# A MoE whose expert blocks add their rows to their tokens' rows in DRAM

## The chip, the cores and the metric

The kernel runs on one core of one Trainium2 chip. The metric is the device time of one execution in microseconds. A core has a matrix engine (TensorE, here PE), a vector engine (VectorE, DVE), an activation engine (ScalarE, ACT), a general engine (GpSimd, POOL) and a sequencer that only starts transfers (SyncE, SP), each with its own instruction queue that runs in order, and 16 DMA engines that all transfers share.

## The reference

Two layers of one trunk work on 768 tokens of width 1024 (256 of context, 512 latent). Each layer has a mixer (a convolution and a state-space scan, in parallel, with one input and one output projection) and then a hierarchical mixture of experts. Only the second is touched by the change:

```python
def hier_moe(h, p):
    g_sel = jnp.argmax(t @ p["w_rg"] + p["b_rg"], axis=-1)          # one of 4 groups
    ...
    top_v, top_i = lax.top_k(jax.nn.softmax(e_logits, axis=-1), MOE_TOPK)   # 2 of 4 experts
    w_sel = g_prob * top_v / jnp.sum(top_v, axis=-1, keepdims=True)
    ...
    def expert(acc, ew):
        wg, wu, wd, cw = ew
        hid = jax.nn.silu(t @ wg) * (t @ wu)
        return acc + (cw[:, None] * (hid @ wd)).astype(acc.dtype), None
```

So each token goes to two of 16 experts, and its two results are added, gated and added to the residual. All data is float32. The second layer's MoE works on the 512 latent tokens alone, and a last RMSNorm gives the output.

## The kernel before

The kernel is written with a framework that puts each engine's instructions in an order by a simulated timeline of its own, and sets the semaphore waits. So the order on an engine follows neither the source alone nor the measured times.

**The expert blocks.** Layer 0 has 768 tokens, layer 1 has 512. A routing stage computes on DVE for each expert the list of its tokens. `CAPS` gives each of the 16 experts a fixed capacity of rows, so that the blocks can be laid out ahead: three experts of a fixed place (128 rows in layer 0, 96 in layer 1) and 13 whose places are filled by the order of their loads (208 down to 48 rows, and 160 down to 40). A block has at most 128 rows; there are 21 blocks with 1936 rows in layer 0 and 17 with 1308 rows in layer 1. What doesn't fit goes through a loop (`tc.For_i(0, nrun)`, L1508), which in this run is entered with zero passes.

For each block an indirect transfer on POOL (`gather`, L1257) brings the tokens' rows of 1024 floats from `h2d` in DRAM, two blocks ahead. PE turns them and multiplies them with the expert's gate and up weights, ACT and DVE apply the SwiGLU and the token's weight, and `down` multiplies with the down weights. Each weight is split in a high and a low part: ACT casts (L1248), and DVE or POOL subtracts (L1249; on POOL for the tiles `C` and `HL`, the second pair of an expert's six pieces). SP loads the six pieces of 512 KB of each expert (`raw`).

**The results.** `down` leaves a block's result `y` in SBUF, and a plain transfer on ACT's queue (L1330) puts it into `ysl`, the list of all result rows in the order of the blocks. Each token has two slots in that list, `slotc`, which the routing computes at its end (`sh`, `row`, `own`: L1410 to L1418). Behind the blocks, `fetch` (L1499) brings for each of the chunks of 128 tokens the two result rows of each token by an indirect transfer on POOL, the second with addition onto the first. In layer 1 both are added in the transfer onto a copy of the residual (ACT L1486). Three of them are issued ahead of the loop (`EARLY`), the others behind it. `combine` multiplies the sum with the gate, adds it to the residual `X1` and stores it (layer 0), or hands it to the last norm (layer 1: ACT L1574, POOL L356, DVE L1576, store L1577). In layer 0 the normed chunks are turned and enter layer 1's input projection (PE L483 to L485), whose weights `wp` SP loads, ACT casts and DVE or POOL subtracts (L465, L466).

**The routing.** DVE puts the token numbers and weights into their places by one-hot products: L1396 and L1399 compare, L1402 multiplies, PE sums (L1406), and `token_weight` (L1219 to L1221) turns that into `idx`, the list that the gathers read. Empty places have token 0 and weight 0.

## Time and profile before

| | |
|---|---|
| times of three runs | 1352.81, 1356.26, 1366.07 us |
| median | 1356.26 us |
| the profiled execution's own time | 1361.08 us |
| its span, first to last instruction | 1359.4 us |
| busy: PE, DVE, ACT, POOL | 80%, 67%, 42%, 44% |
| mean granted clock of PE | 0.902 |
| DMA moved | 258.79 MB, mean 190 GB/s |

The busy shares are averages over stages that are unlike: the mixers, the routing, the expert blocks and the two places where a layer ends. Idle time of an engine is read together with what ended it, which the views put in square brackets behind a row. A DMA's row on POOL or SP is its issue; when its data has landed is told by who waited for it, or by the view of transfers.

### The profile page before, as it was taken

Reading aid. Unit: us, or ns where it says so; the run is one execution under the profiler, and the core shown is the slowest. Engines: PE = TensorE matmul, PEld = TensorE weight load, DVE = VectorE, ACT = ScalarE, POOL = GpSimd, SP = SyncE. Lnnn points to the kernel's source line nnn. Section 1 sums busy time; section 2 is a strip of 40 time slices with the busy share of each in tenths; the row PEclk is TensorE's granted clock in tenths of the full one; section 3 lists DMA queues with packets and bytes.
Section 4 is the critical chain, followed back from the end, with each engine's and each line's share of the span. In section 5 each row is a group of like instructions: output and inputs, shape, how many; then the busy total and the mean of one; then the engine's idle time right before and its main releaser. Section 6 shows DMA issues by size and latency. Waiting matters only on the chain. (4 is left out here: it accounts for less than half of the span.)

```text
span 1359.4 us, 19509 instructions
## 1 busy us (share of the span) xinstructions
...
## 2 busy tenths in 40 slices
...
DMA  8855434513443194999856666022594363989856
GB/s 256 274 164 197 142 106 122 169 48 105 159 131 103 68 333 157 340 351 315 277 186 183 214 189 201 11 68 96 186 328 144 111 196 109 348 298 314 304 157 158
DMA packets 120733, 258.79 MB, mean 190 GB/s; under 512 B 16108, under 2 KB 61786, under 8 KB 115514
## 3 DMA queue, kind: packets, MB, share of 16 engines
...
q10 hardware_dynamic: 7429, 19.89, 3.9%
...
## 5 line engine op out<-in xcount | busy, mean ns | idle before, releaser
L466 POOL TENSOR_TENSOR t<-wp,t 128x1024 fp32r<-128x1024 f32 (+1 forms) x36 | 109.6, 3047 | 134.0 <-ACT t L465 108.8
L724 DVE SCALAR_TENSOR_TENSOR acc<-v,cwcol,acc 128x504 f32<-128x504 f32 (+19 forms) x176 | 136.2, 802 | 0.6
L1249 POOL TENSOR_TENSOR C<-raw,wraw 128x1024 fp32r<-128x1024 f32 x28 | 74.4, 2671 | 113.0 <-ACT wraw L1248 67.5
L483 PE MATMUL mm<-HL,t 128*128 128x512 f32 (+1 forms) x272 | 110.2, 408 | 15.4 <-ACT ad L438 7.1
L1248 ACT CAST wraw<-raw 128x1024 fp32r<-128x1024 f32 x92 | 94.5, 1047 | 43.4 <-DMA raw<-in_w_down_dram 16.3
L485 PE MATMUL mm<-HL,t 128*128 128x512 f32 (+1 forms) x272 | 107.6, 396 | 1.7 <-POOL t L466 1.7
L484 PE MATMUL mm<-HL,t 128*128 128x512 f32 (+1 forms) x272 | 107.3, 395 | 0.2 <-DVE HL L378 0.2
L1249 POOL TENSOR_TENSOR HL<-raw,HL 128x1024 fp32r<-128x1024 f32 x24 | 63.5, 2659 | 78.7 <-ACT HL L1248 78.6
L356 POOL TENSOR_TENSOR rstd<-ms,mhalf 128x1 f32<-128x1 f32 (+3 forms) x29 | 24.3, 838 | 150.4 <-DVE ms L354 150.4
L653 DVE SCALAR_TENSOR_TENSOR t<-t,pcol,t 128x772 f32<-128x772 f32 (+1 forms) x64 | 87.1, 1360 | 2.0
L483 PE MATMUL sm<-wraw,t 128*128 128x256 f32 (+8 forms) x304 | 88.0, 290 | 0.0
L484 PE MATMUL sm<-C,t 128*128 128x256 f32 (+8 forms) x304 | 85.8, 282 | 2.2 <-DVE C L1249 1.9
L485 PE MATMUL sm<-wraw,t 128*128 128x256 f32 (+8 forms) x304 | 85.7, 282 | 0.0
L483 PE MATMUL mm<-t,HL 128*128 128x256 f32 x256 | 76.3, 299 | 8.3 <-ACT t L645 2.6
L1257 POOL DMA_INDIRECT t<-h2d,idx x38 | 55.3, 1456 | 59.0 <-DVE cw L1221 17.1
L465 ACT CAST t<-wp 128x1024 fp32r<-128x1024 f32 (+1 forms) x40 | 42.0, 1053 | 90.5 <-DMA wp<-in_w_in_dram 40.0
L483 PE MATMUL sm<-HL,t 128*128 128x256 f32 (+8 forms) x272 | 78.7, 289 | 1.8 <-ACT HL L1248 1.7
L484 PE MATMUL sm<-HL,t 128*128 128x256 f32 (+8 forms) x272 | 77.2, 284 | 1.9 <-DVE HL L1249 1.9
L485 PE MATMUL sm<-HL,t 128*128 128x256 f32 (+8 forms) x272 | 77.2, 284 | 0.0
L483 PEld LDWEIGHTS mm<-HL,t 128*128 128x128 f32 x272 | 53.8, 199 | 33.3 <-issue 7.4
L485 PE MATMUL mm<-t,HL 128*128 128x256 f32 x256 | 75.0, 294 | 0.1
L484 PE MATMUL mm<-t,HL 128*128 128x256 f32 x256 | 74.5, 292 | 0.0
(472 smaller groups left out, 3388.7 us busy)
## 6 DMA issues: line engine op xcount, KB each, us to landing
...
```

Of the source, the lines that this page charges most:

```text
L356: G.tensor_tensor(r[:, :n], ms[:, :n], mhalf[:, :n], op=OP.pow)
L465: S.copy(hi, t)
L466: eng.tensor_sub(lo, t, hi)
L483: T.matmul(dst, lh, rh, start=(k == 0), stop=False)
L484: T.matmul(dst, lh, rl, start=False, stop=False)
L485: T.matmul(dst, ll, rh, start=False, stop=(k == K8 - 1))
L653: V.scalar_tensor_tensor(xa[:, :n], xpt[:, tap:tap + n], col, xa[:, :n], op0=OP.mult, op1=OP.add)
L724: eng.scalar_tensor_tensor(da, sa, tapc(k, ct), da, op0=OP.mult, op1=OP.add)
L1248: highs.append(S.copy(hi, r))
L1249: eng.tensor_sub(lo, r, hi)
L1257: gathered.append(G.indirect_dma_start(out=xg[:n], out_offset=None, in_=h2d, in_offset=bass.IndirectOffsetOnAxis(ap=icol[:n], axis=0)))
```

## The change

Each block adds its result to its tokens' rows in DRAM at once. `acc_d` has a row for each token, and 128 rows ahead of them for empty places: `idx` now counts from there, so token t is row 128 + t and an empty place of partition p is row p, which no other place of that block has. In layer 0 `acc_d` is filled with zeros while the mixer runs (eight stores of 512 KB on SP, one of them for the empty rows of `h2d`), in layer 1 with the residual `X1` (four stores on SP, when the routing's logits are done). `down` ends in `scatter`, an indirect transfer on POOL with addition. The fetches, `ysl`, `slotc` and the steps that computed it are gone, and `combine` loads a chunk of `acc_d` by a plain transfer on SP. In the loop the result is scattered too, in place of a product that picked tokens, and the weights lie in other tiles.

```diff
     G.iota(tokid[:, 0], pattern=[[0, 6]], base=0, channel_multiplier=1, allow_small_or_imprecise_dtypes=True)
-    G.iota(tokid[:, 1], pattern=[[1, 6]], base=0, channel_multiplier=0, allow_small_or_imprecise_dtypes=True)
+    G.iota(tokid[:, 1], pattern=[[1, 6]], base=1, channel_multiplier=0, allow_small_or_imprecise_dtypes=True)
     zrow = const.tile([P, 8], F32, name="zrow")
...
     av = const.tile([P, 2, 16], F32, name="av")
-    block0, capv, rowsh = [const.tile([P, 2, 16], F32, name=n) for n in ("block0", "capv", "rowsh")]
+    block0, capv = [const.tile([P, 2, 16], F32, name=n) for n in ("block0", "capv")]
     for l in range(2):
...
             G.memset(capv[:, l, j:j + 1], float(n))
-            G.memset(rowsh[:, l, j:j + 1], float(P * b - row))
...
-    slotc = const.tile([P, 2, 6], I32, name="slotc")
+
+    h2d, acc_d = [dram.tile([P + NT, D], F32, name=n) for n in ("h2d", "acc_d")]
     for l in range(2):
...
         ln_fill()
+        if not last:
+            z = main.tile([P, D], F32, name="t4", bufs=8)
+            V.memset(z, 0.0)
+            nc.sync.dma_start(out=h2d[0:P, :], in_=z)
+            for i in range(7):
+                nc.sync.dma_start(out=acc_d[i * P:(i + 1) * P, :], in_=z)
...
                         V.scalar_tensor_tensor(x[h], x[h], self.r[:, j:j + 1], self.sr[:, h], op0=OP.mult, op1=OP.add)
-                        nc.scalar.dma_start(out=h2d[i * P:(i + 1) * P, h * 512:(h + 1) * 512], in_=x[h])
+                        nc.scalar.dma_start(out=h2d[(i + 1) * P:(i + 2) * P, h * 512:(h + 1) * 512], in_=x[h])
...
             pr.norm()
+            if last:
+                for i in (i0, i0 + 1):
+                    nc.sync.dma_start(out=chunk(acc_d, i + 1), in_=X1[:, :, i, :])
         mix_stack.close()
...
         size = [min(P, n - j) for *_, n in items for j in range(0, n, P)]
-        NB, nrow = len(size), sum(size)
+        NB = len(size)
         nblk = NB + M_x
         nst = NB * P
-        ysl = dram.tile([nrow + 1, D], F32, name=f"ysl{l}")
-        nc.sync.dma_start(out=ysl[0:1, :].rearrange("o (p k) -> (o p) k", p=P), in_=zrow)
...
             tid = rt(f"tid{n}", n)
-            V.tensor_scalar(tid, p3[:, :, 1], 128.0, None, op0=OP.mult)
+            V.tensor_scalar(tid, p3[:, :, 1], 0.0, tokid[:, 0, 0:1], op0=OP.is_equal, op1=OP.mult)
+            V.scalar_tensor_tensor(tid, p3[:, :, 1], 128.0, tid, op0=OP.mult, op1=OP.add)
             V.tensor_tensor(idx, tid, p3[:, :, 0], op=OP.add)
...
                 S.copy(y[:n, 512:1024], py[:n, 512:1024])
-            nc.scalar.dma_start(out=ysl[1 + sum(size[:b]):1 + sum(size[:b + 1]), :], in_=y[:n])
+            scatter(y, idx0[:, b:b + 1] if b < NS else idx[:, b:b + 1], n)
+
+        def scatter(y, icol, n=P):
+
+            G.indirect_dma_start(out=acc_d, out_offset=bass.IndirectOffsetOnAxis(ap=icol[:n], axis=0),
+                                 in_=y[:n], in_offset=None, compute_op=OP.add)
...
             V.tensor_copy(eidi, eid)
-            B1, cap, sh = rt("B1", 16), rt("cap", 16), rt("sh", 16)
-            for dst, src in ((B1, block0), (cap, capv), (sh, rowsh)):
+            B1, cap = rt("B1", 16), rt("cap", 16)
+            for dst, src in ((B1, block0), (cap, capv)):
                 V.tensor_mul(sq, PO, src[:, l, None, :].to_broadcast([P, 16, 16]))
...
             nov = rt("nov", 16)
-            V.scalar_tensor_tensor(sq[:, :, :C], tokid[:, 1, None, :C].to_broadcast([P, 16, C]), 128.0,
+            V.scalar_tensor_tensor(sq[:, :, :C], iota128[:, None, :C].to_broadcast([P, 16, C]), 128.0,
                                    tmp[:, :, None].to_broadcast([P, 16, C]), op0=OP.mult, op1=OP.is_lt)
...
             V.tensor_mul(OHS, OH, SL[:, None].to_broadcast([P, 2, C, 16]))
-            slot, row = rt("slot", 2, C), rt("row", 2, C)
+            slot = rt("slot", 2, C)
             V.tensor_reduce(slot, OHS, axis=AX.X, op=OP.add)
...
             V.tensor_copy(rf, ri)
-            return pos, cap, sh, ninc, SL, row, eidi, bf, rf
+            return ninc, eidi, bf, rf
...
             token_weight(pt, nblk, idx, cw)
-            V.tensor_sub(SL, SL, sh[:, None, :].to_broadcast([P, C, 16]))
-            V.tensor_mul(OH, OH, SL[:, None].to_broadcast([P, 2, C, 16]))
-            V.tensor_reduce(row, OH, axis=AX.X, op=OP.add)
-
-            own = rt("own", 2, C)
-            V.tensor_scalar(own, row, float(nrow), None, op0=OP.is_lt)
-            V.scalar_tensor_tensor(own, row, 1.0, own, op0=OP.add, op1=OP.mult)
-            for q, op in enumerate((OP.min, OP.max)):
-                V.tensor_tensor(slotc[:, q, :C], own[:, 0], own[:, 1], op=op)
...
             split_load(1, (V,) * 4, 2, range(4))
-        pos, cap, sh, ninc, SL, row, eidi, bf, rf = slots()
+        ninc, eidi, bf, rf = slots()
         xT = turn(xgs.pop(0), size[0], whole(gu[0]))
...
             prev_i = i
-        bufs = {}
-        if last:
-            xl = main.tile([P, 4, D], F32, name="HL0")
-            with behind(highs[-1]):
-                for c in range(4):
-                    S.copy(halves(xl[:, c]), X1[:, :, c, :])
-                    bufs[c] = xl[:, c]
-        else:
+        if not last:
             grow = row_bcast(l, *[(2, 1, st[4]) for st in act_streams])
-        if last:
-            steps = [(c, 0) for c in range(EARLY[l], 4)] + [(c, 1) for c in range(4)]
-        else:
-            steps = [(c, q) for c in range(4) for q in range(2) if q or c >= EARLY[l]]
-
-        def fetch(i, q, last=last, n=nrow + 1):
-
-            if not last and q == 0:
-                bufs[i] = main.tile([P, D], F32, name="t4", bufs=8) if i >= 4 else moep.tile([P, D], F32, name=f"raw{i}")
-            G.indirect_dma_start(out=bufs[i], out_offset=None, in_=ysl[0:n],
-                                 in_offset=bass.IndirectOffsetOnAxis(ap=slotc[:, q, i:i + 1], axis=0),
-                                 **(dict(compute_op=OP.add) if last or q else {}))
-
-
-        for c in range(EARLY[l]):
-            fetch(c, 0, n=1 + nrow - size[-1])
         down(dn[prev_i], turn_hid(hid, size[-1], False), NB - 1)
...
             e = nc.sync.value_load(ec[0:1, 0:1], min_val=0, max_val=NE - 1)
-            w6 = [main.tile([P, 2, D], F32, name="wraw", bufs=3) for _ in range(3)]
-            w6 = [load_piece(e, j, w6[j // 2][:, j % 2]) for j in range(6)]
+            w6 = [main.tile([P, 4, D], F32, name=f"HL{q}") for q in range(2)]
+            w6 = [load_piece(e, j, w6[j // 4][:, j % 4]) for j in range(6)]
             xT = main.tile([P, K8, P], F32, name="t4", bufs=8)
...
             y = main.tile([P, D], F32, name="t4", bufs=8)
-            V.tensor_copy(y, py)
-            for c0, c1, t0, t1, s in act_streams:
-                for j in range(c0, c1):
-                    pick = moep.tile([P, P], F32, name="pick")
-                    V.tensor_scalar(pick, iota128, icf[:, 0:1], float(-j * P), op0=OP.subtract, op1=OP.is_equal)
-                    py = mm_tile()
-                    for h in range(2):
-                        T.matmul(py[:, h * 512:(h + 1) * 512], pick, y[:, h * 512:(h + 1) * 512], start=True, stop=True)
-                    t = main.tile([P, D], F32, name="t4", bufs=8)
-                    V.tensor_mul(halves(t), halves(py), grow[s])
-                    xc = halves(bufs[j]) if last else X1[:, :, j, :]
-                    V.tensor_add(xc, xc, halves(t))
+            if last:
+                V.tensor_mul(halves(y), halves(py), grow[0])
+            else:
+                V.tensor_copy(y, py)
+            scatter(y, ic[:, 0:1])
...
             xsave = dram.tile([NL, D], F32, name="xsave")
-        def combine(i, last=last):
-            if i >= 4:
-                steps.extend((i, q) for q in range(2))
-            while (i, 1) in steps or (i < 3 and (i + 1, 1) in steps):
-                fetch(*steps.pop(0), last)
-            y = bufs[i]
+
+        def combine(i, last=last, moep=moep, grow=grow):
+            if last or i >= 4:
+                y = main.tile([P, D], F32, name="t4", bufs=8)
+            else:
+                y = moep.tile([P, D], F32, name=f"raw{i}")
+            nc.sync.dma_start(out=y, in_=acc_d[(i + 1) * P:(i + 2) * P, :])
             if last:
```

How the instructions stand now, at three places. First POOL in the middle of layer 0's blocks; `C` and `HL` are weights' low parts, the rows with `h2d` are gathers. Before:

```order
289 L1249 TENSOR_TENSOR C_5954<-raw_5741,wraw 128x1024 [waits DVE_49,DMAHW3_49,PE_49,Activation_49]
290 L1257 DMA t_5850<-h2d_3500,idx 128x1024 [waits DMASW5_49]
291 L1249 TENSOR_TENSOR C_5954<-raw_5745,wraw 128x1024 [waits DMAHW5_49,Activation_49]
292 L1257 DMA t_5982<-h2d_3500,idx 32x1024 [waits DMASW6_49,PE_49]
293 L1249 TENSOR_TENSOR HL_6085<-raw_5965,HL_6084 128x1024 [waits DVE_49,PE_49,DMAHW2_49,Activation_49,Pool_49]
294 L1249 TENSOR_TENSOR HL_6085<-raw_5969,HL_6084 128x1024 [waits DMAHW4_49,Activation_49]
295 L1257 DMA t_6112<-h2d_3500,idx 64x1024 [waits DMASW7_49,PE_49]
```

and now the same stretch, with scatters (`acc_d`):

```order
269 L1255 TENSOR_TENSOR C_5921<-raw_5708,wraw 128x1024 [waits DMAHW7_49,PE_49,Activation_49]
270 L1263 DMA t_5817<-h2d,idx 128x1024 [waits DMASW2_49]
271 L1255 TENSOR_TENSOR C_5921<-raw_5712,wraw 128x1024 [waits DMAHW0_49,Activation_49]
272 L1340 DMA acc_d<-t_5813,idx 896x1024 [waits DMASW1_49,Activation_49]
273 L1263 DMA t_5949<-h2d,idx 32x1024 [waits DMASW4_49,DMASW0_49,PE_49]
274 L1255 TENSOR_TENSOR HL_6052<-raw_5932,HL_6051 128x1024 [waits PE_49,DMAHW5_49,Activation_49,Pool_49]
275 L1255 TENSOR_TENSOR HL_6052<-raw_5936,HL_6051 128x1024 [waits DMAHW6_49,Activation_49]
276 L1340 DMA acc_d<-t_5906,idx 896x1024 [waits DMASW3_49,DVE_49]
277 L1263 DMA t_6079<-h2d,idx 64x1024 [waits DMASW6_49,DMASW2_49,PE_49]
278 L1340 DMA acc_d<-t_6038,idx 896x1024 [waits DMASW5_49,Activation_49]
```

The scatters stand between the gathers and the subtractions. A scatter waits for its block's result (ACT or DVE) and for a software DMA: the numbers 1, 3, 5, 7 go round, and each is the one of the scatter before, as all of them write `acc_d`.

Second, POOL at the end of layer 1: the last subtractions, what follows, and the entry of the loop. Before:

```order
466 L1249 TENSOR_TENSOR C_11874<-raw_11765,wraw 128x1024 [waits DVE_49,DMAHW6_49,PE_49,Activation_49]
467 L1249 TENSOR_TENSOR C_11874<-raw_11769,wraw 128x1024 [waits DMAHW7_49,Activation_49]
468 L1499 DMA HL_11965<-ysl_9649,slotc 128x1024 [waits DMAHW3_49,DMAHW2_49,DMAHW4_49,DVE_49,DMAHW5_49,PE_49,Activation_49]
469 L1499 DMA HL_11965<-ysl_9649,slotc 128x1024 [waits Activation_49] x2
470 L1507 TENSOR_LOAD ebi [waits DVE_49]
471 L1508 COMPARE_AND_BRANCH
472 L1508 ISA [waits DMASW6_49]
```

and now:

```order
459 L1255 TENSOR_TENSOR C_11780<-raw_11671,wraw 128x1024 [waits DMAHW3_49,PE_49,Activation_49]
460 L1255 TENSOR_TENSOR C_11780<-raw_11675,wraw 128x1024 [waits DMAHW4_49,Activation_49]
461 L1340 DMA acc_d<-t_11774,idx 896x1024 [waits DMASW2_49,DVE_49]
462 L1340 DMA acc_d<-t_11867,idx 896x1024 [waits DMASW4_49,DMASW3_49,DVE_49]
463 L1340 DMA acc_d<-t_11890,idx 896x1024 [waits DMASW4_49,DVE_49]
464 L1486 TENSOR_LOAD ebi [waits DVE_49]
465 L1487 COMPARE_AND_BRANCH
466 L1487 ISA [waits DMASW7_49,DMASW6_49]
```

Three fetches ahead of the loop became three scatters, one behind the other; the five fetches behind the loop are gone, and SP has four plain loads of `acc_d` there.

Third, DVE in the routing of layer 1, from the last small step to the product for which PE waits (L1402 before, L1413 now). Before:

```order
1105 L1389 CAST rf<-ri 128x8
1106 L1249 TENSOR_TENSOR C_10209<-raw_9963,wraw 128x1024
1107 L1249 TENSOR_TENSOR C_10209<-raw_9967,wraw 128x1024
1108 L1415 TENSOR_SCALAR own<-row 128x8
1109 L1399 TENSOR_TENSOR ad<-iota_108,bf 128x224
1110 L1396 TENSOR_TENSOR t_9977<-iota_108,rf 128x512
1111 L1396 TENSOR_TENSOR t_9978<-iota_108,rf 128x512
1112 L1285 SCALAR_TENSOR_TENSOR ad<-ad,cw_9777,sm 96x256
1113 L1416 SCALAR_TENSOR_TENSOR own<-row,own 128x8
1114 L1402 TENSOR_TENSOR t_9983<-ad,tv 128x1120
```

and now:

```order
1080 L1400 CAST rf<-ri 128x8
1081 L1410 TENSOR_TENSOR ad<-iota_108,bf 128x224
1082 L1407 TENSOR_TENSOR t_9890<-iota_108,rf 128x512
1083 L1407 TENSOR_TENSOR t_9891<-iota_108,rf 128x512
1084 L1413 TENSOR_TENSOR t_9896<-ad,tv 128x1120
1085 L1255 TENSOR_TENSOR C_10115<-raw_9876,wraw 128x1024
1086 L1255 TENSOR_TENSOR C_10115<-raw_9880,wraw 128x1024
1087 L1291 SCALAR_TENSOR_TENSOR ad<-ad,cw_9691,sm 96x256
```

The two subtractions into `C` moved behind the product, and the two steps of `own` are gone.

## Rows read from the trace of the kernel before

**Rows 1.** Two windows inside the expert blocks of the layers: busy time of engines, granted clock, DMA.

```profile
core 0: us, PE busy (x) PEld busy (x) DVE busy (x) ACT busy (x) POOL busy (x), PEclk, DMA share, GB/s
540.00:700.00 160.00, 156.20 (x1112) 137.95 (x1111) 101.17 (x131) 102.03 (x155) 77.28 (x40) 1.00 0.89 312
...
1160.00:1300.00 140.00, 127.81 (x872) 108.95 (x872) 97.93 (x123) 83.49 (x120) 75.47 (x33) 0.96 0.91 311
```

**Rows 2.** The queue of ACT's DMAs over the whole span, on the page: packets, MB, share of 16 engines.

```profile
q10 hardware_dynamic: 7429, 19.89, 3.9%
```

**Rows 3.** The DMA queues again, of the stretch from 1317 us to 1359.4 us.

```profile
q0 software_dynamic: 1152, 4.19, 54.5%
...
q1 hardware_dynamic: 576, 2.10, 12.1%
```

**Rows 4.** Issue to landing of the gathers of line 1257.

```profile
DMA to landing us min/median/max: 4.2/8.3/14.4
```

**Rows 5.** The same of the fetches of line 1499.

```profile
DMA to landing us min/median/max: 5.6/7.9/11.8
```

**Rows 6.** Timeline of ACT, stores of results in both layers: start, length, line, operation.

```profile
535.28 0.35 ACTq L1330 DMA_DIRECT2D ysl<-t  x1
...
723.81 0.31 ACTq L1330 DMA_DIRECT2D ysl<-t  x1
...
727.50 0.31 ACTq L1330 DMA_DIRECT2D ysl<-t  x1
...
1150.40 0.33 ACTq L1330 DMA_DIRECT2D ysl<-t  x1
...
1319.81 0.29 ACTq L1330 DMA_DIRECT2D ysl<-t  x1
```

**Rows 7.** The longest waits of POOL in the window 540 to 700: total, times, longest.

```profile
POOL HL L1249 <- ACT HL L1248: 38.1, 8, 12.0
```

**Rows 8.** The end of layer 1 in the chain of waits: start, length, what.

```profile
1320.91 9.56 DMA HL<-ysl,slotc
...
1339.79 10.44 DMA HL<-ysl,slotc
```

**Rows 9.** The end of layer 1 in the timeline of all engines.

```profile
1332.36 1.56 POOL L1499 DMA_INDIRECT HL<-ysl,slotc  x1 [9.91 <-issue]
...
1353.30 1.28 DVE L1576 SCALAR_TENSOR_TENSOR t<-HL,rstd,bigA 128x1024 f32<-128x1024 f32 x1 [0.44 <-POOL rstd L356]
```

**Rows 10.** From layer 0 to layer 1, timeline of POOL, DVE and PE.

```profile
737.49 1.60 POOL L1499 DMA_INDIRECT raw<-ysl,slotc  x1 [7.46 <-issue]
...
743.79 1.23 DVE L1561 TENSOR_TENSOR raw<-raw,wraw 128x1024 f32<-128x1024 f32 x1 [3.63 <-DMA raw<-ysl,slotc]
...
764.11 1.23 DVE L1561 TENSOR_TENSOR raw<-raw,wraw 128x1024 f32<-128x1024 f32 x1 [5.39 <-DMA raw<-ysl,slotc]
...
768.30 0.58 PE L483 MATMUL mm<-HL,t 128*128 128x256 f32 x1 [7.14 <-ACT ad L438]
```

**Rows 11.** Routing of layer 1, timeline of DVE, POOL and PE.

```profile
1130.76 4.50 DVE L1249 TENSOR_TENSOR C<-raw,wraw 128x1024 fp32r<-128x1024 f32 x2 [0.83 <-PE sm L484]
...
1135.19 2.30 DVE L1415 TENSOR_SCALAR own<-row 128x8 f32<-128x8 f32 x1
...
1130.87 6.60 POOL L1249 TENSOR_TENSOR C<-raw,wraw 128x1024 fp32r<-128x1024 f32 x2 [22.55 <-PE sm L485]
...
1142.55 0.97 POOL L1257 DMA_INDIRECT t<-h2d,idx  x1 [5.08 <-DVE ov L1434]
...
1140.74 0.51 PE L1406 MATMUL mm<-t,t 128*128 128x140 bf16 x3 [9.90 <-DVE t L1402]
```

**Rows 12.** Routing of layer 0, timeline of DVE and PE.

```profile
519.52 2.34 DVE L1416 SCALAR_TENSOR_TENSOR own<-row,own 128x12 f32<-128x12 f32 x1
...
524.05 1.82 PE L1406 MATMUL mm<-t,t 128*128 128x165 bf16 x12 [4.66 <-DVE t L1402]
```

**Rows 13.** The DMA engines in the 40 slices of the page, 34 us each, in tenths.

```profile
DMA  8855434513443194999856666022594363989856
```

2 lines of the change are left out of this document (removed).

## The prediction

> **What bounds the kernel now.** I read the stages one after the other, since the change touches four kinds of place that have different limits. The windows of the expert blocks come first [rows 1]: TensorE (PE) is busy 156.2 of 160 us in layer 0 and 127.8 of 140 us in layer 1, while the 16 DMA engines are busy 0.89 and 0.91 of the time. So PE sets the pace there, and DMA has 0.11 x 160 = 17.6 and 0.09 x 140 = 12.6 us of room left. The stores of the blocks' results give the pace: in layer 0 the first is at 535.28 and the last, 20 blocks later, at 727.50, which is 9.6 us a block; in layer 1 16 blocks later, 10.6 us a block [rows 6].
>
> Behind the blocks nothing but transfers moves. In the chain of waits the end of layer 1 is two DMA pieces of 9.56 and 10.44 us [rows 8], with five issues on POOL between them, the first at 1332.36 [rows 9]. Between the layers the first fetch behind the loop is issued at 737.49, VectorE (DVE) gets the first token chunk at 743.79 and the fourth at 764.11, and the in-projection of layer 1 starts at 768.30 [rows 10]. Ahead of the blocks stands the routing, where PE waits for DVE: 9.90 us in layer 1 [rows 11] and 4.66 us in layer 0 [rows 12].
>
> **The end of layer 1: removed fetches, added scatters and loads.** Eight fetches of 512 KB that add in the transfer go. In their place the last scatter must land before the loop is entered, and then four plain loads of 512 KB come. The last result is ready at 1319.81 [rows 6]. For the last scatter (40 rows) I take the shortest fetch, 5.6 us [rows 5], so it lands at 1325.4, not at 1330.47 where the early fetches landed [rows 8]. From there to the first instruction behind the loop it took 1.9 us (1332.36 - 1330.47); now 1327.3. No row shows the landing of a lone plain load of 512 KB; the nearest is the last output store, from 1353.30 + 1.28 [rows 9] to the end at 1359.4, 4.8 us. Further loads follow at their data time: the output stores took 12.1% of 42.4 us for 2.10 MB, 2.44 us per MB [rows 3], so 1.3 us each. The fourth lands at 1327.3 + 4.8 + 3.9 = 1336.0, where the last fetch landed at 1350.23. What follows (ACT, DVE until 1354.58, the store) stays 1359.4 - 1350.23 = 9.2 us, a little more because four chunks now arrive 1.3 us apart and each needs ACT and 1.28 us of DVE. That is **-13 us**, between -9 (the scatters before it are late) and -14.
>
> **Between the layers.** The last five scatters of layer 0 stand in a row on POOL. The last result is there at 727.50; the scatter before it belongs to a result of 723.8 [rows 6], lands 5.6 us later at 729.4, and the last at 735.0. With the 1.9 us of the loop the loads start at 736.9: as late as the fetch at 737.49. The first chunk is there at 741.7 instead of 743.79, but the fourth at 745.6 and not at 764.11. The in-projection can't use all of it: DVE has some 4 x 2.5 us for the chunks and the weights' subtractions beside it, about 16 us from the first chunk on, so it would start at 757.5 at best, 11 us earlier. Behind it PE depends on weights that the same DMA engines bring. I take half, **-6 us**, between -2 and -11.
>
> **The routing.** In layer 1 two weight subtractions (4.50 us) and the `own` step (2.30 us) stand ahead of the products of L1402, for which PE waits; the order after has the subtractions behind and no `own`. That is 6.8 us, but POOL's subtractions (from 1130.87, 6.60 us) keep POOL from its first gather until 1137.5, against 1142.55 [rows 11]: 5 us. So **-5 us** (-3 to -7). The delayed subtractions feed an expert that PE reaches after the projections of the block at hand, so I cost their delay at nothing; without that cover it is 4.5. In layer 0 `own` goes ahead of L1402 (2.34 us, of PE's 4.66 us) and the `slotc` steps behind it [rows 12]: **-3 us** (-2 to -5).
>
> **The price of the addition.** A plain store of a result costs DMA 3.9% of 1359.4 us for 19.89 MB, 2.67 us per MB [rows 2]. The eight adding fetches at the end, alone on their queue, took 54.5% of 42.4 us for 4.19 MB, 5.51 us per MB [rows 3]. The blocks of layer 0 have 1936 rows, 7.93 MB, those of layer 1 1308 rows, 5.36 MB. So DMA has 7.93 x 2.84 = 22.5 us more to do beside the blocks of layer 0 and 15.2 us in layer 1. Against 17.6 and 12.6 us of room that is just too much if all of it were used; but PE, not DMA, is at its limit, weights are loaded some blocks ahead, and the stretch after the last weight load has more room. I take about a quarter, **+6 and +4 us**; the ends are 0 and 22.5 and 15.2.
>
> **The chain of scatters.** Each scatter waits for the one before it to land, and POOL stands still at that wait, with the gather of a later block and the next expert's subtractions behind it. A gather under this load lands in 8.3 us (4.2 to 14.4) [rows 4]. A block of layer 0 has 92 rows or 0.38 MB on average, so the addition makes it 8.3 + 0.38 x 2.84 = 9.4 us, just under the 9.6 us between blocks; in layer 1 (77 rows) it is 9.2 us against 10.6. POOL idles for ACT's casts anyway (38.1 us in 8 waits in the window, 12.0 at most [rows 7]), and a wait for a landing that falls into these costs nothing. I take **+2 us** in all; the dear end is a rival below. The Trainium skill ("DMA: Bandwidth & Descriptors", "Anatomy of one DMA — SWDGE (gpsimd) path") gives a transfer from GpSimd 2.0 us and its bytes at 436 GB/s, which would be an estimate of 2.9 us for such a block plain, and the chain could then never hold POOL; the trace does not agree, its least gather took 4.2 us [rows 4].
>
> **The rest.** Eight zero stores of 512 KB in layer 0 stand on SP's queue ahead of the scan's small loads; 8 x 1.3 = 10 us of DMA in a stretch (272 to 340 us) whose slices show 1 and 3 tenths of DMA [rows 13]: +1 us, 0 to +4. The 2 MB of copied residual in layer 1 (5 us of DMA at the same rate), no longer added on ACT at the end, lie some 50 us ahead of the weights that PE wants next: nothing, at worst +2. ACT loses four copies and 38 store issues, DVE about nine small steps a layer, which hide behind PE.
>
> **The sum.** -13 - 6 - 5 - 3 + 6 + 4 + 2 + 1 = -14 us. The profiled execution took 1361.08 us (span 1359.4), so 1347 us in its terms; it lay 4.8 us above the median of the three runs, 1356.26, and from there the forecast is **1342 us**.
>
> **Rivals.** *The chain of scatters becomes the bound* (slower). If a scatter lands in 12 us, still inside the gathers' own 4.2 to 14.4 [rows 4], then each block of layer 0 comes 2.4 us later, 20 x 2.4 = +48, because gathers and subtractions wait behind it on POOL. Layer 1, with smaller blocks and 10.6 us between them, gets about nothing from it. With the gains (-27) and the smaller terms (+7) that gives 1384 us. It decides from a landing of 9.6 us, and my mean is 9.4: against it speaks that a slower pace also empties the DMA engines, for it that the first blocks have 128 rows.
>
> *DMA is full* (about 1370 us): all of the 22.5 and 15.2 us come out on the path, since a PE that is 98% busy can't make up a late weight: -27 + 38 + 3. For it speaks a share of 0.9 before anything is added. The rule that an addition costs two reads and thus half of the rate is in the Trainium skill ("Collectives: The Full Stack", "The bandwidth ceiling: the fold count and why AG ≠ RS ≠ AR"), said there of ReduceScatter; 5.51 against 2.67 us per MB [rows 2, 3] is that or a little worse.
>
> *The additions are hidden altogether* (about 1329 us): PE's pace stays, the costs are nothing, and the gains of 27 us remain.
>
> *The ends don't get shorter* (about 1356 us): the scatters at the ends land so late that the loop is entered no earlier, and the plain loads give back only what the additions cost. The change then has moved the wait from fetches to scatters and doesn't shorten what it is about.
>
> **How the numbers follow.** Forecast 0.38, of which half beyond 1% (this kernel's measurement tells about 1%, 13.6 us, from no change); additions hidden 0.15; DMA full 0.15; chain of scatters 0.22; ends no shorter 0.10. Faster by over 1%: the hidden case, half of the forecast and the earlier share of the case between, 0.40. Slower: the chain and a part of full DMA, which lies on the border, 0.27. The rest, 0.33, is the same. The range leaves out the better half of the hidden case and the worse half of the chain: 1328 to 1380; the forecast by itself is 1332 to 1352.
>
> **What will show it.** Right: the scatters land in under 9.6 us, POOL's idle time in the blocks stays with ACT's casts, the first to last result of layer 0 stays near 192 us, the loop of layer 1 is left some 5 us sooner after the last result, and the last input chunk lands within 10 us of that. Wrong: POOL idle until a scatter lands, PE waiting for DVE's or POOL's weights or for gathers, a DMA share near 1.0 in all windows of the blocks with PE below 19 of 20 us, or an in-projection that starts earlier and then waits for weights.

## The result, and the profile after

The change made the kernel faster: a median of 1316.79 us in four runs, against 1356.99 us for four of the kernel before on the same chip. The ratio is 0.9693 (95% interval 0.9638 to 0.9748), so some 40 us were gained where 14 were forecast and 1328 was the best end of the range. The profiled execution took 1313.54 us, with a span of 1311.8 us. It lies 3.3 us below its median and that of before 4.1 us above its own, so the difference of the two spans, 47.6 us, is some 7 us more than that of the medians.

Both traces, cut at the same events. The events are the first `down` product and the last result of each layer, the first matmul of layer 1's in-projection, and the transposes ahead of layer 1's router:

| stretch | before | after | difference | the prediction's terms for it |
|---|---|---|---|---|
| start to first `down` product, layer 0 | 525.7 | 524.9 | -0.8 | -3 (routing) +1 (zero stores) |
| to the last result of layer 0 | 200.5 | 198.2 | -2.3 | +6 (addition) +2 (chain) |
| to the in-projection of layer 1 | 42.1 | 30.9 | -11.2 | -6 |
| to the router of layer 1 | 284.2 | 276.1 | -8.0 | none |
| to the first `down` product of layer 1 | 89.2 | 75.6 | -13.5 | -5 |
| to the last result of layer 1 | 176.9 | 175.6 | -1.2 | +4 (addition) |
| to the end of the span | 40.9 | 30.4 | -10.5 | -13 |

So the prediction's costs don't show in the rows of the blocks, two of its gains were too small, and a third, ahead of the router, had no term. A second profile of the changed kernel, below, repeats the middle five rows within 1.6 us. But kernels of the experiments that are alike in a stretch can differ by more: they have 521.2 to 529.4 us in the first row and 198.2 to 202.7 us in layer 0's blocks, so the -0.8 and the -2.3 us say nothing.

**The blocks.** The same two kinds of window as in [rows 1], in the kernel after:

```profile
core 0: us, PE busy (x) PEld busy (x) DVE busy (x) ACT busy (x) POOL busy (x), PEclk, DMA share, GB/s
540.00:700.00 160.00, 159.56 (x1139) 142.30 (x1138) 102.86 (x132) 101.94 (x155) 107.17 (x56) 0.99 0.99 315
1125.00:1270.00 145.00, 133.06 (x926) 113.57 (x926) 103.60 (x130) 86.08 (x126) 104.76 (x47) 0.99 0.98 314
```

DMA went from 0.89 to 0.99, and PE, at 156.20 of 160 us before, is busy for 159.56. The second profile of the changed kernel has the same DMA share in that window and less of PE:

```profile
540.00:700.00 160.00, 154.87 (x1112) 137.28 (x1111) 101.58 (x127) 100.42 (x151) 103.95 (x54) 1.00 0.99 313
```

So nearly all the room of DMA was used, and PE is as busy as before within 3.4 us. The scatters and the gathers, issue to landing, and how long POOL stood still for a scatter's landing (total, times), in the view of each line's instructions:

```profile
DMA to landing us min/median/max: 4.6/8.1/11.5
...
DMA to landing us min/median/max: 5.0/8.1/9.5
...
  DMA acc_d<-t,idx: 23.0, 5
```

A scatter that adds lands about as soon as a plain gather, at a median of 8.1 us each (8.8 and 8.0 in the second profile), below the 9.6 us from which the chain would decide. Of the 38 scatters only 5 found POOL waiting for the one before, and three of these stand at the ends of the layers (8.46, 4.24 and 3.94 us); the two in the blocks waited 6.3 us together.

**Between the layers.** Timelines of POOL, SP, DVE and PE in the kernel after:

```profile
727.67 1.36 POOL L1340 DMA_INDIRECT acc_d<-t,idx  x1 [4.24 <-DMA acc_d<-t,idx]
...
732.38 1.88 SPq L1531 DMA_DIRECT2D raw<-acc_d  x4
...
735.99 2.50 DVE L1534 TENSOR_TENSOR raw<-raw,wraw 128x1024 f32<-128x1024 f32 x2
...
741.81 1.22 DVE L1534 TENSOR_TENSOR raw<-raw,wraw 128x1024 f32<-128x1024 f32 x1
...
754.01 0.39 PE L481 MATMUL mm<-HL,t 128*128 128x256 f32 x1 [1.27 <-ACT ad L436]
```

The four loads go out in 1.88 us, and DVE multiplies the four chunks from 735.99 to 743.0 without a wait for one, where it took from 743.79 to 765.3 before [rows 10].

**The end.** The chain of waits after, from the last two scatters on, and the timeline of SP and ACT there:

```profile
1279.57 4.58 DMA acc_d<-t,idx
1284.95 4.58 DMA acc_d<-t,idx
1291.33 5.36 DMA t<-acc_d
1298.03 4.21 DMA t<-acc_d
1304.69 1.28 DVE t L1549
```

```profile
1290.46 1.28 SPq L1531 DMA_DIRECT2D t<-acc_d  x3
1297.65 0.34 SPq L1550 DMA_DIRECT2D out_dram<-t  x1
1298.03 0.43 SPq L1531 DMA_DIRECT2D t<-acc_d  x1
...
1302.32 1.06 ACT L1547 ACTIVATE t<-t 128x1024 f32<-128x1024 f32 x1 [4.41 <-DMA t<-acc_d]
```

The two pieces of 9.56 and 10.44 us [rows 8] became pieces of 5.36 and 4.21 us. But the fourth load stands behind an output store on SP, which waits for the first chunk's norm, so it starts 7.6 us after the first of the other three.

**The price of the addition.** The queue of POOL's transfers over the whole span, on the page of the kernel after and then of the first experiment, which scatters without addition:

```profile
q0 software_dynamic: 8032, 27.14, 9.0%
```

```profile
q0 software_dynamic: 8032, 27.14, 6.1%
```

The same 27.14 MB take 0.090 x 1311.8 = 118 us of all 16 engines with addition and 0.061 x 1305.1 = 80 us without. The 38 us between are what the prediction put on DMA (22.5 + 15.2; the capacities in `CAPS` add up to 1376 rows for layer 1 and not to 1308, which makes it 22.5 + 16.0). The size was right; what the path sees of it is the question of the first experiments.

### The profile page after: what moved, and what is told of

Same layout as the page of the kernel before. It is cut to its first block, busy times and chain, and to the rows that moved or that the text cites. A ratio compares the mean times of both kernels' runs of the same rounds, so it can differ in the third digit from the quotient of the medians.

```text
span 1311.8 us, 19492 instructions
## 1 busy us (share of the span) xinstructions
PE 1069.5 (82%) x7103; PEld 876.6 (67%) x7103; DVE 905.5 (69%) x1350; ACT 572.2 (44%) x1017; POOL 628.2 (48%) x467
## 3 DMA queue, kind: packets, MB, share of 16 engines
q0 software_dynamic: 8032, 27.14, 9.0%
## 5 line engine op out<-in xcount | busy, mean ns | idle before, releaser
L723 DVE SCALAR_TENSOR_TENSOR acc<-v,cwcol,acc 128x448 f32<-128x448 f32 (+19 forms) x176 | 131.4, 777 | 0.6
L481 PE MATMUL mm<-HL,t 128*128 128x512 f32 (+1 forms) x272 | 109.0, 403 | 10.5 <-ACT t L463 6.2
L1254 ACT CAST wraw<-raw 128x1024 fp32r<-128x1024 f32 x92 | 95.1, 1047 | 39.6 <-DMA raw<-in_w_up_dram 12.0
L1340 POOL DMA_INDIRECT acc_d<-t,idx x38 | 70.5, 1855 | 78.1 <-DMA acc_d<-t,idx 23.0
L483 PE MATMUL mm<-HL,t 128*128 128x512 f32 (+1 forms) x272 | 105.6, 388 | 2.2 <-POOL t L464 2.2
L482 PE MATMUL mm<-HL,t 128*128 128x512 f32 (+1 forms) x272 | 106.5, 392 | 0.0
L481 PE MATMUL sm<-wraw,t 128*128 128x256 f32 (+8 forms) x304 | 87.4, 288 | 1.7 <-ACT t L1284 1.6
L1263 POOL DMA_INDIRECT t<-h2d,idx x38 | 50.0, 1316 | 53.3 <-PE sm L1239 16.6
```

What stands on the lines that cost most here:

```text
L481: T.matmul(dst, lh, rh, start=(k == 0), stop=False)
L482: T.matmul(dst, lh, rl, start=False, stop=False)
L483: T.matmul(dst, ll, rh, start=False, stop=(k == K8 - 1))
L723: eng.scalar_tensor_tensor(da, sa, tapc(k, ct), da, op0=OP.mult, op1=OP.add)
L1254: highs.append(S.copy(hi, r))
L1263: gathered.append(G.indirect_dma_start(out=xg[:n], out_offset=None, in_=h2d, in_offset=bass.IndirectOffsetOnAxis(ap=icol[:n], axis=0)))
```

## The experiments

The theory from here on: in the blocks the additions and the chain cost nothing, and the gain is that of plain loads at the ends, of the context chunks, and of another order in the routing. Its rivals: the costs are there and larger gains cover them; the gain of the routing is that of the removed `slotc` steps; and the whole shift of 8 us in the mixer is the clock.

**The changed kernel again**, for the spread of its stretches.

> The changed kernel once more, beside the others of this group. Theory H (the additions and the chain of scatters are hidden; the gain comes from the two ends, the context's chunks and the routing): 0.969 of the kernel before. Theory C (the additions do cost some 10 us beside the blocks, and the gains elsewhere are larger still) gives the same here; the run only sets the level for the other three.

Measured 1318.20 us, ratio 0.9692 (0.9656 to 0.9729). Stretches 2 to 7 of the table are 199.4, 31.2, 276.1, 74.1, 174.4 and 29.4 us. Differences under 2 us in one profile are not read below, and in layer 0's blocks and the stretch ahead of them none within the spreads given above.

**Scatters without addition**, everything else as in the change.

```diff
-                                 in_=y[:n], in_offset=None, compute_op=OP.add)
+                                 in_=y[:n], in_offset=None)
```

> The scatters write their rows and don't add them (the sum of a token's two results and the residual is left out), so the DMA engines have less to do and all waits stay. Theory H: within 3 us of the changed kernel, since PE sets the pace in the blocks; the ends win at most 1 to 2 us, as the last scatters land sooner. Theory C: 8 to 15 us faster than the changed kernel, most of it in the windows of the blocks.

Measured 1306.64 us, 0.9596 (0.9564 to 0.9629). That is 11.6 us below the second run of the changed kernel (1318.20), where theory H gave at most 3 and theory C 8 to 15. But the blocks, in which theory C wanted most of it, don't show it: layer 0's took 197.3 us (198.2 and 199.4 in the two profiles with addition), layer 1's 178.3 (175.6 and 174.4; its tokens are others here, as layer 0's result differs). The addition costs something where nothing hides it: the stretch between the layers is 28.6 us (30.9 and 31.2), the end 26.9 us (30.4 and 29.4). That is some 5 us of the 11.6. Of the others 3.4 us lie, between this profile and the second one of the change, ahead of the first scatter, where the two kernels are alike, and 2.1 us in the mixer; what they come from isn't shown. The landing of the plain scatters, 1.0 and 1.7 us sooner than the two medians with addition, and the window in layer 0's blocks:

```profile
DMA to landing us min/median/max: 2.5/7.1/11.3
...
540.00:700.00 160.00, 159.14 (x1142) 142.01 (x1141) 102.01 (x132) 101.69 (x156) 95.83 (x56) 0.99 0.90 315
```

DMA is busy 0.90 instead of 0.99 for the same 315 GB/s and the same PE. A share of 0.99 is thus no sign here that DMA binds.

**The same in layer 1 alone**, so that both layers work on the right tokens up to the last sum.

```diff
-                                 in_=y[:n], in_offset=None, compute_op=OP.add)
+                                 in_=y[:n], in_offset=None, **({} if last else dict(compute_op=OP.add)))
```

> Scatters write plainly in layer 1 alone (the sum of the residual and two results is left out there), so the routing is that of the changed kernel and no extra block runs. If the additions cost nothing on the path: the blocks of layer 1 take 174 to 177 us as in the changed kernel, and the end wins 2 to 3 us. If they cost: 5 to 10 us fewer in the blocks.

Measured 1311.55 us, 0.9648 (0.9597 to 0.9699). The blocks of layer 1 take 175.5 us, against 175.6 and 174.4; the end is 27.0 us, 3.4 and 2.4 shorter. With the right tokens, then, layer 1's blocks show no cost of the addition.

**Four destinations in turn**, so that a scatter waits for the fourth before it and not for the last.

```diff
+    accs = [acc_d] + [dram.tile([P + NT, D], F32, name=f"acc{n}") for n in range(3)]
...
-            G.indirect_dma_start(out=acc_d, ...
+            G.indirect_dma_start(out=accs[(NB - 1 - b) % 4], ...
```

> The scatters add into four buffers in turn, of which only one is read at the end (the sum over the other three is left out), so each scatter waits for the fourth before it and not for the last. Theory H: within 3 us; POOL's idle time until a scatter lands (23 us in 5 waits) falls to nearly nothing but the blocks take as long as before, and the end of a layer wins up to 5 us a layer because the last scatters overlap. Theory C with the chain as its cost: 10 us or more faster, in the blocks.

Measured 1345.21 us, 0.9902 (0.9863 to 0.9941), but this time says nothing: layer 0's other result routes layer 1 otherwise, and the loop made a pass (a gather of L1264 at 1293.90, its scatter at 1316.35). Layer 0 can be read: 199.4 us for the blocks, where the change has 198.2 and 199.4. Freed from the chain they are no faster.

**The same in layer 1 alone.**

```diff
+            G.indirect_dma_start(out=accs[(NB - 1 - b) % 4 if last else 0], ...
```

> Scatters of layer 1 add into four buffers in turn, of which one is read (three quarters of the sum are left out), so a scatter waits for the fourth before it. If the chain costs in the blocks: 3 to 6 us fewer there, most of it in the first ones, where a gather stands behind a scatter that had not landed (6.2 us of POOL). If not: 174 to 177 us, and only the end wins, 2 to 4 us.

Measured 1324.35 us, 0.9751 (0.9682 to 0.9821); blocks of layer 1 178.2 us, end 28.8. Freed from the chain, layer 1's blocks are no faster either, and the end gains 0.6 to 1.6 us, less than the 2 to 4 that were expected.

**Each scatter twice**, so that a block needs two links of the chain.

```diff
+            G.indirect_dma_start(out=acc_d, out_offset=bass.IndirectOffsetOnAxis(ap=icol[:n], axis=0),
+                                 in_=y[:n], in_offset=None, compute_op=OP.add)
```

> Each scatter is issued twice, so that every result is added twice (the experts' part of the output is doubled): twice the additions, twice the chain. Theory H says how much room there is: DMA stood at 0.99 in layer 0's blocks, so this goes beyond it, and the chain of two landings of 8 us a block against 9.6 us between blocks must bind: 100 us or more slower. Theory C: the same sign, but growing from the first scatter on; what tells them apart is whether one chain (8.1 us) already left POOL idle.

Measured 1528.54 us, 1.1235 (1.1198 to 1.1272). Layer 0's blocks take 255.8 us (+57.6), the stretch behind them 91.2 (+60.3), layer 1's blocks 206.0, and its end 90.6. The first and the last of layer 0's 42 scatters on POOL, and POOL's waits for a landing ahead of the first and of the second of a pair:

```profile
536.63 2.01 POOL L1340 DMA_INDIRECT acc_d<-t,idx  x1 [3.50 <-ACT t L1335]
...
846.43 1.35 POOL L1342 DMA_INDIRECT acc_d<-t,idx  x1 [2.87 <-DMA acc_d<-t,idx]
...
  DMA acc_d<-t,idx: 101.2, 26
...
  DMA acc_d<-t,idx: 104.6, 28
```

That is (846.43 - 536.63) / 41 = 7.6 us a link, a pace that the landings set: 205.8 us of waits in place of 23.0. So the rival's mechanism exists; a block with two links needs 15.1 us, more than the 9.6 that PE gives it, while one with one link fits.

**Fetches instead of loads for the two context chunks.** In the changed kernel each of the two chunks is brought by a pair of indirect transfers again (an empty one and an adding one), as before.

```diff
...
-            nc.sync.dma_start(out=y, in_=acc_d[(i + 1) * P:(i + 2) * P, :])
+            if i >= 4:
+                pair(y, i)
+            else:
+                nc.sync.dma_start(out=y, in_=acc_d[(i + 1) * P:(i + 2) * P, :])
```

> The two context chunks at the end of layer 0 come as before by two indirect transfers on POOL each (the first brings rows of zeros, the second adds the token's row), everything else as changed. Theory H: the 8 us that the stretch from layer 1's input projection to its router became shorter were these four fetches, which stood on POOL behind waits for PE and ahead of weight subtractions; they come back, +6 to +9 us against the changed kernel. Rival S (that stretch only became shorter because the order of the filler work on DVE and the start state of that stage differ): within 3 us.

Measured 1326.29 us, 0.9726 (0.9688 to 0.9765). The stretch from in-projection to router took 278.8 us, 2.6 more than in the change. That lies within the 3 us of rival S and not in the 6 to 9 us of theory H; the nine profiles with plain loads there have 274.0 to 277.0 us. Layer 1's blocks took 181.3 us here, 5.7 more than in the change, which wasn't followed up.

**Fetches for layer 0's four latent chunks**, with three of them ahead of the loop as before, and then **fetches at the end of layer 1** (a pair for each chunk, again an empty one and an adding one). The core of both edits:

```diff
+                while (i, 1) in steps or (i < 3 and (i + 1, 1) in steps):
+                    c, q = steps.pop(0)
+                    fetch(c, q, acc_d if q else h2d)
+                y = bufs[i]
```

> The four latent chunks at the end of layer 0 come by a fetch on POOL ahead of the loop (rows of zeros) and an adding fetch behind it, everything else as changed. Theory H: the 11 us from the last result of layer 0 to layer 1's input projection come back in large part, +6 to +11 us, since adding fetches land some 3 us apart. Rival L (that part was won because the loop is entered sooner): nearly nothing comes back, below 3 us, since the loop is entered as soon as in the changed kernel.

> The end of layer 1 with fetches: four of rows of zeros ahead of the loop and four adding ones behind it, in place of four plain loads; all else as changed. Theory H: +5 to +9 us (the kernel before took 12 us longer from the last result to the end, of which some 3 us belong to the loop being entered later). Rival L: below 3 us.

The first: 1339.19 us, 0.9821 (0.9768 to 0.9875). The stretch between the layers is 40.5 us again, 9.6 more than in the change, and the one to the router 279.2, 3.1 more. The second: 1329.26 us, 0.9756 (0.9723 to 0.9788), with an end of 36.0 us, 5.6 more. In both, layer 1's blocks took some 10 us longer in the profile (185.8 and 186.7) though no line of the blocks was changed. With the fetches between the layers a gather there stood behind a scatter's landing on POOL, and PE then waited for its rows:

```profile
1145.88 1.27 POOL L1267 DMA_INDIRECT t<-h2d,idx  x1 [8.68 <-DMA acc_d<-t,idx]
...
1154.76 1.52 PE L1277 MATMUL tp<-ident,t 128*128 128x128 f32 x6 [4.14 <-DMA t<-h2d,idx]
```

It waits because its tile is one that a scatter still reads. With the fetches at the end the two waits are 9.00 and 4.89 us. The changed kernel has such a wait of POOL too, of 6.16 us (at 1121.08), but no wait of PE for those rows. The other part is the granted clock. The blocks of layer 1 with fetched latent chunks, and in the changed kernel:

```profile
1122.87:1308.57 185.70, 164.17 (x1064) 135.34 (x1061) 122.74 (x153) 95.48 (x139) 120.50 (x56) 0.94 0.86 268
...
1105.80:1281.40 175.60, 159.90 (x1061) 130.80 (x1061) 121.69 (x152) 95.74 (x139) 121.53 (x56) 0.98 0.90 284
```

PE needs 4.3 us more for the same products, at 0.94 instead of 0.98, and stands idle for 5.8 us more. So the chain can reach the path by that buffer, with some 4 to 5 of the 10 us.

The clock and PE's work in the first two stretches of 40 us from the in-projection on, before, after, with fetched context chunks and with fetched latent chunks:

```profile
768.30:808.30 40.00, 40.00 (x238) 34.02 (x239) 27.87 (x38) 13.89 (x21) 12.11 (x8) 0.95 0.41 138
808.30:848.30 40.00, 31.65 (x154) 20.58 (x153) 40.00 (x51) 9.25 (x13) 20.20 (x10) 0.87 0.67 198
```

```profile
754.01:794.01 40.00, 40.00 (x246) 33.71 (x247) 29.24 (x38) 14.11 (x21) 10.01 (x4) 1.00 0.48 155
794.01:834.01 40.00, 33.08 (x188) 22.99 (x187) 39.65 (x56) 11.65 (x17) 18.72 (x10) 0.96 0.54 182
```

```profile
760.00:800.00 40.00, 40.00 (x246) 33.71 (x247) 29.24 (x38) 14.11 (x21) 13.52 (x7) 1.00 0.49 154
800.00:840.00 40.00, 31.54 (x159) 20.75 (x158) 40.00 (x54) 9.24 (x13) 18.55 (x10) 0.87 0.67 204
```

```profile
770.75:810.75 40.00, 40.00 (x239) 33.99 (x240) 27.98 (x36) 13.89 (x21) 9.97 (x4) 0.96 0.48 157
810.75:850.75 40.00, 32.95 (x177) 22.88 (x176) 39.66 (x55) 11.74 (x17) 20.14 (x10) 0.94 0.55 182
```

The fetches of the latent chunks bring back the first row of before (0.96, so part of that time was at 1.2 and not at 2.4 GHz; 239 matmuls instead of 246). Those of the context chunks bring back the second (PE 31.5 of 40 us, DVE busy throughout; the 0.87 says less, as the second profile of the change has 0.91 there, with 32.94 us of PE). The length of PE's pause ahead of the first row is not the reason for its clock: with doubled scatters the stretch ahead is 91.2 us and the row has 1.00 all the same:

```profile
873.90:913.90 40.00, 40.00 (x246) 33.71 (x247) 29.24 (x38) 14.11 (x21) 10.05 (x4) 1.00 0.45 147
```

What differs in the rows is that PE gets the chunks piecemeal when they are fetched: before, its transposes there begin at 752.52, 754.92 and 760.00, with waits between, and with loads the first 24 run from 747.31 to 752.74 with one wait of 0.17 us. That this sets the clock wasn't tested.

**The kernel before with plain loads** in place of its fetches: no additions, no scatters, and what it loads are rows of `ysl` that don't belong to the tokens.

```diff
...
-            while (i, 1) in steps or (i < 3 and (i + 1, 1) in steps):
-                fetch(*steps.pop(0), last)
-            y = bufs[i]
...
+            nc.sync.dma_start(out=y, in_=ysl[r:r + P, :])
```

> The kernel before, with its plain stores of results and all steps of the routing, but with one plain load a chunk on SP in place of the fetches (each brings the last 128 result rows; the second result of a token and, in layer 1, the residual are left out of the sum). It has the ends of the changed kernel without a single addition. Theory H (the ends and the context's chunks carry the gain, the additions cost nothing): 0.978 of the kernel before, that is -30 us: -11 to -13 at each end and up to -8 in the stretch from the input projection to the router. Rival S (that stretch and the routing became shorter by other things than the fetches): -22 to -24 us, with the stretch at 282 to 285 us and the routing at 88 to 90 as before.

Measured 1319.53 us, 0.9695 (0.9638 to 0.9752). Between the layers 28.1 us (14.0 less than before), to the router 280.7 (3.5 less, but the five variants of the kernel before that don't touch this stretch have 282.6 to 289.9), routing 89.4 (nothing), layer 1's blocks 171.9 (5.0 less), end 23.4 (17.5 less). Against this kernel the change's last scatters, with addition, keep back 3 us between the layers and 7 at the end. The whole is 39.6 us faster than the kernel before, where the theory gave 30.

**The kernel before without the steps of `slotc`** (`sh`, `row`, `own`; the slots are a plain count).

> The kernel before without the steps that compute slotc (a fixed list of rows takes its place, so the fetches bring other rows of the same size). Theory H: in layer 1 the stretch from the router to the first down product falls from 89 us by about 5 (own is gone, but the subtractions into C still stand ahead of the last product in this order), in all -5 to -8 us with layer 0. Rival G (most of the 13 us there came from gathers that were issued sooner, a 5.6 us issue of the second gather before, and not from the steps): within 3 us unless that issue is short by chance, in which case PE waits 6 us less for it.

Measured 1350.46 us, 0.9929 (0.9899 to 0.9960); routing of layer 1 87.4 us, 1.8 less. These steps are little of the 13.5. The whole is 8.7 us faster, and layer 1's blocks take 171.6 us, 5.3 less. So in the kernel before these blocks got some 5 us shorter both without these steps and without the fetches. The changed kernel has neither, and 175.6 us. Some 4 us that the scatters cost there, and the other removals cover, are thus not excluded; taking away the addition (175.5 us) or the chain (178.2 us) didn't bring them out.

**The kernel before with its first four DVE subtractions later**, behind the first slot steps and no longer ahead of them.

```diff
-                V.tensor_reduce(dst, sq, axis=AX.X, op=OP.add)
+                red = V.tensor_reduce(dst, sq, axis=AX.X, op=OP.add)
+            with behind(pr.last_copy, routed, red):
+                split_load(1, (V,) * 4, 2, range(4))
...
-        with behind(pr.last_copy, routed):
-            split_load(1, (V,) * 4, 2, range(4))
```

> The kernel before, with the first four weight subtractions of DVE (into C) behind the first steps of the slot computation, as the changed kernel has them; nothing is removed. Theory D (DVE's four subtractions in a row hold up POOL's issue of a gather that runs beside them): in layer 1 the issue of the second gather falls from 5.6 us to about 1, PE's wait of 6 us for it goes, and the stretch becomes 5 to 6 us shorter; 0.996 of the kernel before. Rival T (the long issue has nothing to do with DVE): it stays above 4 us and the stretch at 89.

First the place in the kernel before, timeline of POOL, DVE and PE:

```profile
1101.52 5.59 POOL L1257 DMA_INDIRECT t<-h2d,idx  x1 [0.30 <-DVE cw L1221]
...
1101.27 4.61 DVE L1249 TENSOR_TENSOR C<-raw,wraw 128x1024 fp32r<-128x1024 f32 x4
...
1116.06 0.88 PE L1267 MATMUL tp<-ident,t 96*128 96x96 f32 x4 [5.98 <-DMA t<-h2d,idx]
```

and in this experiment:

```profile
1110.16 1.04 POOL L1257 DMA_INDIRECT t<-h2d,idx  x1 [0.30 <-DVE eidi L1354]
...
1133.42 5.50 POOL L1249 TENSOR_TENSOR C<-raw,wraw 128x1024 fp32r<-128x1024 f32 x2 [21.00 <-PE sm L485]
...
1133.27 3.45 DVE L1398 TENSOR_TENSOR t<-iota,rf 128x512 bf16<-128x512 f32 x2
1136.64 2.30 DVE L1418 SCALAR_TENSOR_TENSOR own<-row,own 128x8 f32<-128x8 f32 x1
...
1140.11 2.35 DVE L1249 TENSOR_TENSOR C<-raw,wraw 128x1024 fp32r<-128x1024 f32 x2
...
1140.23 1.09 PE L1408 MATMUL mm<-t,t 128*128 128x140 bf16 x8 [6.84 <-DVE t L1404]
```

Before, the issue of the second gather took 5.59 us and ended 1.2 us after DVE's four subtractions in a row, which ran beside it (4.61 us), and PE then waited 5.98 us for its rows. With the subtractions behind the issues these take 1.04 and 0.92 us, and that wait is gone; PE's wait for the product is 6.84 us and not 9.90 [rows 11]. The routing stage is 80.0 us, 9.2 less than before, and these two waits make up 9.0 of it. The median, 1353.82 us, 0.9951 (0.9921 to 0.9981), shows little of it: in the profiled execution other stretches were longer (the first by 5.6 us).

What is left of the change's gain is the wait for the product, 6.84 us here and 1.43 in the change:

```profile
1101.66 1.29 DVE L1407 TENSOR_TENSOR t<-iota,rf 128x512 bf16<-128x512 f32 x2
...
1104.23 0.66 PE L1417 MATMUL mm<-t,t 128*128 128x140 bf16 x8 [1.43 <-DVE t L1413]
```

It was first sought in the order again, by moving two more subtractions behind the product (`cw_ins` holds the step that reads it, the sum into `cw`):

```diff
...
-                split_load(i + 1, (V, V, G, G, V, V), expert(i + 2) if i + 2 < NE else None)
+                with behind(*([cw_ins[0]] if i == 2 else [])):
+                    split_load(i + 1, (V, V, G, G, V, V), expert(i + 2) if i + 2 < NE else None)
```

> As e10, and the next two subtractions into C behind the product for which PE waits, in both layers; the slotc steps stay. Theory D with the order as the whole cause: 13 to 15 us fewer in that stretch of layer 1, PE's wait for the product falls from 9.9 to 1 to 3 us, and the time is 0.989 to 0.991 of the kernel before. If the own steps matter beside it, 2 to 5 us of that are missing.

That failed: 1355.83 us, 0.9990 (0.9966 to 1.0014), stage 80.4 us, and PE's wait still 6.84 us. But the rows of the run before it show the holder: the `own` step of 8 columns ends at 1138.94, when POOL's two subtractions end (1133.42 + 5.50 = 1138.92), and the two compares ahead of it take 3.45 us where the change has 1.29. In [rows 11] it is the same: `own` ends at 1137.49, POOL's subtractions at 1137.47, and DVE's own two subtractions take 4.50 us beside them, where the two at 1140.11 above take 2.35. So the next two runs take away either side: `own` and its like, with the new order, and POOL's subtractions, given to DVE behind the product.

```diff
-                    split_load(i + 1, (V, V, G, G, V, V), ...
+                    split_load(i + 1, (V,) * 6 if i == 2 else (V, V, G, G, V, V), ...
```

> The kernel before, without the slotc, row and own steps (the slots are a plain count, so it fetches other rows and its output differs) and with the four DVE subtractions behind the first slot steps. Theory A (POOL's pair of subtractions into C, 5.5 us from 1133.42, stretches whatever DVE runs beside it, so the two compares still take 3.45 us and only the 2.30 us of the own step go): the wait of PE for the product is 6.84 - 2.3 = 4.5 us and the routing stage 80.0 - 2.3 = 77.7 us, about 2 above the changed kernel's 75.6. Theory B (the own steps are nothing and their 2.30 us move to the next step): 80.0 us and a wait of 6.8. Theory C (own and order are all of it): wait 1.4, stage 75.6.

> The kernel before with the four DVE subtractions behind the first slot steps, and the first pair of subtractions that POOL would do in the routing of layer 1 (and of layer 0) given to DVE, behind the product. Nothing is left out. Theory A (POOL's subtraction stretches DVE's steps): the two compares take 1.29 us and not 3.45, each own step under 0.3 us and not 2.30, the wait of PE for the product falls from 6.84 to 2.4 us, and the routing stage from 80.4 to 76 us. Theory B (these steps are slow for another reason): they stay at 3.45 and 2.30 us and the wait at 6.8. The total is expected at 0.99 to 1.0 by both, as DVE has two more subtractions (2.3 us) behind the product.

The rows of the second of them, where the `own` steps are all still there:

```profile
1118.34 1.29 DVE L1399 TENSOR_TENSOR t<-iota,rf 128x512 bf16<-128x512 f32 x2
1119.55 0.16 DVE L1419 SCALAR_TENSOR_TENSOR own<-row,own 128x8 f32<-128x8 f32 x1
...
1120.99 0.66 PE L1409 MATMUL mm<-t,t 128*128 128x140 bf16 x8 [2.56 <-DVE t L1405]
```

With POOL quiet the compares take 1.29 us, an `own` step 0.16, and PE waits 2.56 us: theory A, for each of its numbers (1.29, under 0.3 and about 2.4). The stage is 74.9 us, 0.7 below the changed kernel's 75.6, and the whole kernel before gains by these two moves alone: 1338.59 us, 0.9860 (0.9816 to 0.9904), more than any theory gave it; the stage is 14.3 of these 19.9 us. The run without `own` has 1344.21 us, 0.9904 (0.9878 to 0.9931), and a stage of 78.0 us. That is the 77.7 that theory A named, but not by its mechanism: POOL's subtractions began only at 1126.54 there, behind the compares, which took 1.28 us.

**All four loads at the end ahead of the first output store.**

```diff
-    for i in range(4):
-        xf = combine(i)
+    xfs = [combine(i) for i in range(4)]
+    for i, xf in enumerate(xfs):
```

> The changed kernel with all four loads at the end of layer 1 written ahead of the first output store; in the changed kernel the fourth load stands on SP behind an output store that waits for the norm (issued at 1298.03, 6.7 us after the third). Both theories: -3 to -5 us, as the fourth chunk is the last that is waited for.

SP's timeline at the end:

```profile
1288.11 1.76 SPq L1531 DMA_DIRECT2D t<-acc_d  x4
1295.55 5.62 SPq L1550 DMA_DIRECT2D out_dram<-t  x4
```

Measured 1311.45 us, 0.9648 (0.9615 to 0.9681): the best version with the full computation, though its interval overlaps that of the change. Its end takes 27.2 us, 3.2 less than the change's and 2.2 less than that of the second run of the change.

## Why the prediction was wrong

The direction and the likeliest sign were right, the size wasn't: -14 us forecast, -40 measured, outside the range. By its own steps:

- **The costs (+6, +4, +2).** They failed as one: nothing of them appears in the rows of the blocks, within their spread. The addition's 38 us of DMA were sized right (but for the 1308 rows, which are 1376), and so was the room of 17.6 and 12.6 us in the windows; but the step "I take about a quarter" had no row behind it. Plain and adding scatters differ by 0.1 us in layer 1's blocks on the same tokens. The prediction itself named what may cover them, weights that are loaded some blocks ahead; how far that cover reaches wasn't measured. In the blocks this is the rival "the additions are hidden altogether"; its 1329 us kept the other terms and so missed too. The additions aren't free, though: without them the whole kernel is 11.6 us faster, some 5 us of it at the two ends, and the rest isn't placed. What a scatter costs layer 1's blocks in other ways stays open, up to some 4 us.
- **The chain of scatters.** The threshold (9.6 us) fits the runs, and the estimate of 9.4 for a landing was too high: 8.1 and 8.8. It added 1.1 us for the addition to a gather's landing. Against a plain scatter (7.1) the addition does take 1.0 to 1.7 us; against a gather it is 0 to 0.8. The doubled scatters show the rival at work, at 15.1 us a block. The way by which the chain did come near the path, a gather that waits for a tile that a scatter reads, the prediction didn't have.
- **Between the layers (-6).** The step "I take half" failed. The end that it gave as best, 11 us, is what happened: the fourth chunk was there in time, weights were not late behind it, and fetches put 9.6 us of it back.
- **The mixer (no term).** The context chunks, fetched from 800.40 on before and loaded at 783.00 now, were not in the sum, nor was PE's start there. Fetching them again gives back 2.6 us, fetching the latent chunks 3.1, both not far outside the spread of 274.0 to 277.0 us. If the two add, 2.3 of 8.0 us stay open. Why the kernel before with plain loads regains only 3.5 us there is open too, though with variants of it at 282.6 to 289.9 us the 8.0 itself is known to a few us only.
- **The routing of layer 1 (-5).** The prediction read the 4.50 us of subtractions and the 2.30 us of `own` as DVE's own work. They were in good part each engine waiting for the other: the subtractions are 2.35 us of work and `own` is 0.16. And it looked only at the product, not at the gathers 30 us ahead, where a POOL issue of 5.59 us was the same thing the other way round. The new order removed both: 6.0 us at the gathers and 3.1 at the product by DVE's subtractions coming later, and the rest by POOL's coming behind the compares. That this needs no step to be left out is shown in the kernel before (74.9 us), where POOL's two went to DVE. The Trainium skill states a rule for it ("SBUF — State Buffer", "Who interferes with whom"): the port pair that DVE shares with GpSimd is an exclusive lock, and a DVE instruction with two inputs in SBUF contends for it with a GpSimd instruction that reads SBUF. The rows of POOL's subtractions agree, with 2.30 against 0.16 us for the two-input `own` step. The same section of the Trainium skill reports a probe in which a `tensor_tensor`, which the subtractions are, did not stall DMA; the issue of this indirect gather, 5.59 against 1.04 us, doesn't agree, and here the measurement decides.
- **The routing of layer 0 (-3) and the zero stores (+1).** -0.8 us measured, where like kernels differ by up to 8; neither can be told.
- **The end of layer 1 (-13).** -10.5 us, inside its bounds. The loads landed faster than reckoned (first chunk at ACT 3.8 us after the issue). The last scatter waited 3.94 us for the one before, and the fourth load stood behind a store on SP, which the sum, with four loads in a row, left out; 2 to 3 us of it come back by the new order of the loads.
